# A decoder layer on one core: the triangular solve's transfers on other queues, and the solve one value tile later

## The chip, the cores and the metric

One Trainium2 chip, one of its cores. The metric is the device time of one execution in microseconds. The engines: TensorE (PE, with PEld for its weight loads), VectorE (DVE), ScalarE (ACT), GpSimd (POOL) and SyncE (SP), which here only issues transfers. Each engine works through its own list of instructions in order, and a transfer is issued by the engine in whose list it stands: an issue that has to wait holds up everything behind it in that list.

## The reference

One decoder layer over 256 tokens of width 2048, in float32. What the change touches is the RWKV-7 scan over 16 heads of width 64, and the rest stands around it.

```
h = rms_norm(x)
proj = h @ w_in                          # 2048 -> 4448 columns
r, k, v, w, a, g = split(token_shift(proj[:3360]))
# for each head, token by token:
sa    = state @ a_t                      # a = -kk, b = kk * a
state = state * w_t + sa b_t^T + v_t k_t^T
y_t   = state @ r_t
y = group_norm(y) + bonus;  y = y * g    # 16 groups of 64
y_mla = latent attention on the other columns (c_q, c_kv, k_pe)
x = x + concat(y, y_mla) @ w_out
x = x + gated MLP with a width-3 convolution (2048 -> 5632 -> 2048);  rms_norm
```

## The kernel before

All large products are done in two float32r parts: `piece` loads a 512 KB weight block by SP (`raw`, three buffers), ACT rounds it to `hi` (L133), DVE subtracts to get `lo` (L134), and PE multiplies both (L163 with `hi`, L166 with `lo`). A tile of the input projection (`in_tile`) is two such halves of 8 + 8 matmuls into one of three product banks `mm`. `joined` empties a bank: a copy on ACT (L171), an add on DVE (L172) and a scale on DVE (L173). The bank is free for PE behind L172.

The input projection runs tile by tile: key tiles 1 to 8, receptance tiles 9 to 16, value tiles 17 to 24, then latent tiles 27 to 34 (`latent`, two times four). A list `pend` holds small steps that are called after a tile, or after one more tile.

The scan is done in four chunks of 64 tokens. For each chunk and head a unit triangular system of 64 x 64 has to be inverted, which the kernel does for all 64 systems together, by halves of 32. `gram` builds the Gram blocks `G1` (PE L524, DVE L529) and stores the 32 x 32 diagonal blocks in DRAM (`dL`, 32 stores of 16 KB, L537). `solve_load` reads them back with one block row a partition (`Lp`, 512 KB, L566). `solve` multiplies `Lp` by the key norms (L575), and then solves on DVE with 31 steps of a multiply and an add (L579, L581) between which other DVE work stands. The inverse `Tq` goes to DRAM as `dT` (L583), its transposed copy `tp` as `dU` (L590), and from there back in the layouts that PE needs: `T11` (two loads, L592, in the profile `T`) and `TT` (four loads, L596); each of these has 1024 runs of 128 bytes. PE then makes the off-diagonal blocks: `pR` from `T11` and `G1` (L625), DVE scales it to `RT` (L629), `pT` from `RT` and `TT` (L638), copied back into `TT` (L642). Behind that comes the chain of chunks (`chunk`), whose matmuls `px`, `py`, `pS` (L674) alternate with small DVE and ACT steps, and which the scheduler fills up with the last latent tiles and the latent attention's products. Each half of the tokens then has a `group_norm`.

`rsqrt` runs on POOL unless an engine is given: 14 instructions there (L201 to L216), 11 on DVE. The group norms use it with 16 columns, `latent` with 2 (`ssm` L774, `rr` L776), behind the sum of squares `pss` (PE L772).

The order within each engine is made by a scheduler, which goes by its own costs and takes the program's order as a first wish; `tc.issue_after(i)` puts an instruction behind instruction i on its engine's list or by a wait.

Of the kernel before, what the change touches and what calls it, by code (L numbers as in the profile page):

```python
# [9 lines left out]
F32 = mybir.dt.float32  # L10
# [4 lines left out]
ALU = mybir.AluOpType  # L15
AX = mybir.AxisListType

P = 128
# [7 lines left out]
GN_EPS = 64e-5  # L26
# [28 lines left out]
def hybrid_layer(ctx: ExitStack, tc: tile.TileContext, a: dict, out: bass.AP):  # L55
    nc = tc.nc
    V, S, PE = nc.vector, nc.scalar, nc.tensor
# [4 lines left out]
    dr = ctx.enter_context(tc.tile_pool(name="dr", bufs=1, space=bass.MemoryType.DRAM))  # L62
# [3 lines left out]
    def nm(s):  # L66
        uid[0] += 1
        return f"{s}{uid[0]}"
# [28 lines left out]
    def ch(n="ch"):  # L97
        return ps.tile([P, 512], F32, tag="ch", name=nm(n), bufs=NCH)
# [4 lines left out]
    def con(shape, n, dt=F32):  # L103
        return sb.tile(shape, dt, name=n, bufs=1)
# [10 lines left out]
    def vv(name, i, rows=slice(0, P)):  # L115
        return vec[rows, VOFF[name] + i:VOFF[name] + i + 1]
# [28 lines left out]
                                               h.bitcast(F32), ALU.mult, ALU.subtract).ins  # L145
        return raw

    last_w, last_lo, last_x = [None], [None], [None]
    pend = []


    def flush(every=False):
        now = [f for n, f in pend if n == 0 or every]
        pend[:] = [(n - 1, f) for n, f in pend if n > 0 and not every]
        for f in now:
            f()
# [32 lines left out]
    def in_tile(i, pf=mm):  # L189
        acc = pf()  # L190
        for h in range(2):
            prod_b(acc, piece(a["win"][i, h]), x_hl, h * 8, 8, h == 0, h == 1)
        flush()
        return acc
# [174 lines left out]
    def shifted(acc, i, rows=slice(0, P), dst=None):  # L369
        h = t1("h", 257)  # L370
        nc.gpsimd.memset(h[rows, 0:1], 0.0)
        joined(h[rows, 1:257], acc, rsB, rows)
        o = t1("sh") if dst is None else dst
        S.activation(o[rows], h[rows, 1:257], AF.Copy, scale=om_mu[rows, i:i + 1])
        V.scalar_tensor_tensor(o[rows], h[rows, 0:256], vv("mu", i, rows), o[rows], ALU.mult, ALU.add)
        return o


# [65 lines left out]
    for p in range(8):  # L444
        pp, g = p // 2, p % 2
# [23 lines left out]
    Mp = con([P, 32], "Mp")  # L469
# [21 lines left out]
    dL = dr.tile([P, 32, 32], F32, name="dL")  # L491
    dLv = dL.rearrange("(h b c p) i t -> b c i h p t", h=2, b=2, c=4)
    boP = ch("boP")
    bon = con([64, 64], "bon")
    for p in range(8):
        pp, g = p // 2, p % 2
        acc = in_tile(9 + p)
        if p == 0:
            pend.append((0, key_norms_p))
        r = shifted(acc, 9 + p)  # L500
        rc = r.rearrange("p (c t) -> p c t", t=64)
        V.tensor_tensor(AR[pp][:, g, :, 1, :], rc, AR[pp][:, g, :, 1, :], ALU.mult)
        pr = t1("pr")
        V.tensor_tensor(pr.rearrange("p (c t) -> p c t", c=4), kv_(pp, g), AR[pp][:, g, :, 1, :], ALU.mult)

        def bonus(p=p, pr=pr):
            for w in range(2):
                PE.matmul(boP[:, w * 16 + p * 2:w * 16 + p * 2 + 2], pr[:, w * P:(w + 1) * P], brk[:, p, :],
                          start=True, stop=True)

        def gram(p=p, pp=pp):
            hf = p // 4
            e0 = (pp % 2) * 2
            for c in range(4):
                if pp % 2 == 0:
                    G1[c].append(s4(n="G1").rearrange("p (e t) -> p e t", e=8))
            for w in range(2):
                pg = [ch("pg") for _ in range(2)]
                for r in range(2):
                    for gg in range(2):  # L520
                        o = (r * 2 + gg) * P
                        for h in range(2):
                            hs = slice(h * 64, h * 64 + 64)
                            PE.matmul(pg[h][:, o:o + P], BK[pp][hs, gg, w * 2 + r, :, :],  # L524
                                      AR[pp][hs, gg, w * 2 + r, :, :], start=o == 0, stop=True,
                                      skip_group_check=True)
                for h in range(2):
                    for r in range(2):
                        V.tensor_tensor(G1[w * 2 + r][hf][:, h * 4 + e0:h * 4 + e0 + 2, :],  # L529
                                        pg[h][:, r * T:(r + 1) * T].rearrange("p (q t) -> p q t", q=2),  # L530
                                        gmask.unsqueeze(1).broadcast_to([P, 2, P]), ALU.mult)
            if pp % 2 == 1:
                for c in range(4):
                    for b in range(2):
                        r0 = 64 + b * 32
                        for h in range(2):
                            nc.sync.dma_start(dLv[b, c, :, h, hf * 4:hf * 4 + 4, :],  # L537
                                              G1[c][hf][r0:r0 + 32, h * 4:h * 4 + 4, b * 32:(b + 1) * 32])
            for c in range(3):
                if pp == 0:  # L540
                    BKt.append(s4(n="BKt").rearrange("p (a t) -> p a t", a=8))
                pt = ch("pt")
                for gg in range(2):
                    PE.transpose(pt[:, gg * P:(gg + 1) * P],
                                 BK[pp][:, gg, c, :, :].rearrange("p s t -> p (s t)"), ident)
                S.copy(BKt[c][:, pp * 2:pp * 2 + 2, :], pt[:, 0:T].rearrange("p (a t) -> p a t", a=2))

        pend.append((0, bonus))
        if g == 1:
            pend.append((0, gram))  # L550
# [8 lines left out]
    TT = con([P, 32, 64], "TT")  # L559
    T11 = []  # L560

    Lps = []

    def solve_load():
        Lps.append(sv("Lp").rearrange("p (i t) -> p i t", i=32))
        nc.sync.dma_start(Lps[0], dL)  # L566

    def solve():
        Lp = Lps[0]
        Tq = sv("Tq").rearrange("p (s t) -> p s t", s=32)  # L570
        tm = t1("tm")
        nc.gpsimd.memset(Tq, 0.0)
        nc.gpsimd.memset(Tq.rearrange("p s t -> p (s t)")[:, 0:1024:33], 1.0)
        nc.gpsimd.memset(TT, 0.0)
        V.tensor_tensor(Lp, Lp, Mp.unsqueeze(1).broadcast_to([P, 32, 32]), ALU.mult)  # L575
        for i in range(31):
            n, m = i + 1, 31 - i
            tv = tm[:, 0:n * m].rearrange("p (s t) -> p s t", s=n)
            V.tensor_tensor(tv, Tq[:, 0:n, i:i + 1].broadcast_to([P, n, m]),  # L579
                            Lp[:, i:i + 1, i + 1:32].broadcast_to([P, n, m]), ALU.mult)  # L580
            V.tensor_tensor(Tq[:, 0:n, i + 1:32], Tq[:, 0:n, i + 1:32], tv, ALU.add)  # L581
        dT = dr.tile([P, 32, 32], F32, name="dT")
        nc.sync.dma_start(dT, Tq)  # L583
        tp = sv("tp").rearrange("p (s t) -> p s t", s=32)
        V.tensor_copy(tp, Tq.rearrange("p s t -> p t s"))
        dU = dr.tile([2, 32, 32, 32], F32, name="dU")
        for h in range(2):
            T11.append(sv("T11").rearrange("p (q s) -> p q s", q=32))
        for h in range(2):
            nc.sync.dma_start(dU[h], tp[h * 64:h * 64 + 32])  # L590
        for h in range(2):
            nc.sync.dma_start(T11[h][64:96], dU[h].rearrange("q s t -> s q t"))  # L592
        for h in range(2):
            for b in range(2):
                k0 = h * 64 + b * 32
                nc.sync.dma_start(TT[k0:k0 + 32, :, b * 32:(b + 1) * 32], dT[k0:k0 + 32].rearrange("q s t -> s q t"))  # L596

    pend.append((0, solve_load))
    pend.append((1, solve))


    UV = [s4(n="UV").rearrange("p (e t) -> p e t", e=8) for _ in range(4)]
# [2 lines left out]
    for pp in range(4):  # L605
        vt = []
        for g in range(2):
            vt.append(shifted(in_tile(17 + pp * 2 + g), 17 + pp * 2 + g))
        pt = ch("pv")
        for g in range(2):  # L610
            for w in range(2):
                PE.transpose(pt[:, (g * 2 + w) * P:(g * 2 + w + 1) * P], vt[g][:, w * P:(w + 1) * P], ident)
        ptv = pt.rearrange("p (g w t) -> p g w t", g=2, w=2)
        for w in range(2):
            for r in range(2):
                S.copy(UV[w * 2 + r][0:64, pp * 2:pp * 2 + 2, :], ptv[r * 64:r * 64 + 64, :, w, :])
# [95 lines left out]
    def group_norm(w):  # L712
        y = yt[w]
        y3 = y.rearrange("p (h v) -> p h v", h=16)
        mu = st("gmu", 16)
# [4 lines left out]
        S.activation(sq, y, AF.Square)  # L720
        va = st("gva", 16)
        V.tensor_reduce(va, sq.rearrange("p (h v) -> p h v", h=16), AX.X, ALU.add)
        rv = rsqrt(va, 1.0 / 64, GN_EPS, 16)
        V.tensor_tensor(y3, y3, rv.unsqueeze(2).broadcast_to([P, 16, 64]), ALU.mult)
        V.tensor_tensor(y, y, gnwb[0], ALU.mult)
        V.tensor_tensor(y, y, gnwb[1], ALU.add)
# [165 lines left out]
    for half in range(2):  # L892
# [3 lines left out]
        for c in range(4):  # L896
# [9 lines left out]
            if half == 1:  # L906
# [3 lines left out]
                for j in range(2):  # L910
                    pt = ch("pxT").rearrange("p (k t) -> p k t", k=2)
                    for k in range(2):
                        for tb in range(2):
                            o = (j * 2 + k) * P
# [34 lines left out]
    for blk, nf in enumerate((24, 20)):  # L949
# [33 lines left out]
        for c in range(4):  # L983
            accs = [mm() for _ in range(2)]
            for i in range(n - (4 if blk == 1 and c == 3 else 0)):
                prod_a(accs, piece(a["wdn"][c, f0 // 2 + i]), h_hi, h_lo, i * 2, 2, i == 0, i == n - 1)
                if blk == 1 and i == 2:
                    q = n - 4 + c
                    held.append((q, piece(a["wdn"][3, f0 // 2 + q], a8("wt"))))
            for tb in range(2):  # L990
# [7 lines left out]
                o = tb * 4 + c  # L998
# [88 lines left out]
```

## Time and profile before

| | |
|---|---|
| median of 3 runs | 1209.64 us (1208.44 to 1210.07) |
| the profiled execution | 1207.02 us |
| its span in the trace | 1205.2 us |
| mean granted clock of TensorE | 0.987 |
| PE busy | 1161.3 us, 96% |
| DVE busy | 837.3 us, 69% |
| ACT busy | 598.2 us, 50% |
| POOL busy | 58.3 us, 5%, 206 instructions |
| moved by POOL's queue (software_dynamic) | 384 packets, 0.75 MB |
| the longest wait of PE | 7.3 us, a product (L163) on an eviction (L172) |

The profile is of one execution. A line of the timeline gives the start and the duration in microseconds, the engine, the source line, the operation with its output and inputs, how many there are together, and in brackets how long the engine had been idle and what ended the idle time. SPq, POOLq and ACTq are those engines' issues of transfers. A row of the waits has the total, the number and the longest.

### The profile page before, as it was taken

How to read it: one execution, taken by the hardware profiler on the slowest of the kernel's cores; microseconds unless marked ns; L12 is line 12 of the kernel's file. 1: busy time of each engine (PE TensorE's matmuls, PEld its weight loads, DVE VectorE, ACT ScalarE, POOL GpSimd, SP SyncE). 2: the span in 40 equal slices, each digit the busy share in tenths (PEclk: the TensorE clock that was granted, in tenths of full speed). 3: DMA queues.
4: the chain of work that ended last, by engine and by line, in shares of the span. 5: the costliest groups of instructions: out<-in, count | busy, mean ns of one | idle time of the engine just before them, and what ended most of it. 6: DMA issues, size and time to landing. Idle time of an engine off the chain costs nothing.

```text
span 1205.2 us, 18442 instructions
## 1 busy us (share of the span) xinstructions
PE 1161.3 (96%) x6993; PEld 992.1 (82%) x6993; DVE 837.3 (69%) x1360; ACT 598.2 (50%) x939; POOL 58.3 (5%) x206
## 2 busy tenths in 40 slices
PE   7899988998799999999999999999999999999996
PEld 6788877887677888888888888888888888888885
DVE  7798759977887556777777776444577777775563
ACT  6784435533444455655555554333355555554451
POOL 1500100011110001000000000000000000000000
PEclk9999998998899999999999999999999999999998
DMA  8544454654133555555555555555655555566661
GB/s 329 177 151 153 144 141 145 204 151 145 54 126 120 191 176 175 194 192 192 192 193 192 193 191 181 193 194 190 204 193 193 192 190 190 190 218 209 209 221 76
DMA packets 71017, 215.82 MB, mean 179 GB/s; under 512 B 17616, under 2 KB 17872, under 8 KB 70928
## 3 DMA queue, kind: packets, MB, share of 16 engines
q1 hardware_dynamic: 69776, 211.84, 53.5%
q10 hardware_dynamic: 768, 2.05, 0.5%
q8 instruction: 55, 0.90, 0.3%
q0 software_dynamic: 384, 0.75, 0.3%
q14 instruction: 34, 0.28, 0.1%
HBM read 210.48 MB, written 3.41 MB: 177 GB/s over the span
## 4 chain that ended last, share of the span: by engine, by line
PE 88%; DVE 7%; POOL 2%; issue 1%; DMA 1%; ACT 0%; SPq 0%; ACTq 0%; DVEq 0%; POOLq 0%
PE mm L163 36%; PE mm L166 18%; PE mm L185 9%; PE mm L183 9%; PE mm L184 9%; DVE lo L134 1%; PE pg L524 1%; PE py L674 1%; PE px L674 1%; POOL sinR L292 0%; DMA raw<-in_win 0%; DMA Lp<-dL 0%; POOL cosR L288 0%; DVE tw L415 0%; PE pS L674 0%
## 5 line engine op out<-in xcount | busy, mean ns | idle before, releaser
L134 DVE TENSOR_TENSOR lo<-raw,hi 128x1024 fp32r<-128x1024 f32 x376 | 460.3, 1225 | 286.6 <-ACT hi L133 277.5
L133 ACT CAST hi<-raw 128x1024 fp32r<-128x1024 f32 x376 | 395.0, 1051 | 458.0 <-issue 250.2
L163 PE MATMUL mm<-z,hi 128*128 128x512 f32 x1408 | 351.3, 392 | 0.0
L163 PEld LDWEIGHTS mm<-z,hi 128*128 128x128 f32 x1408 | 251.9, 188 | 43.7
L166 PEld LDWEIGHTS mm<-z,lo 128*128 128x128 f32 x1408 | 188.3, 188 | 14.5
L166 PE MATMUL mm<-z,lo 128*128 128x256 f32 x1408 | 191.6, 278 | 0.0
L163 PE MATMUL mm<-x,hi 128*128 128x512 f32 x528 | 142.2, 406 | 20.0 <-DVE h L172 12.0
L184 PE MATMUL mm<-lo,hh 128*128 128x512 f32 x336 | 130.7, 389 | 0.0
L185 PE MATMUL mm<-hi,hl 128*128 128x512 f32 x336 | 130.7, 389 | 0.0
L163 PEld LDWEIGHTS mm<-x,hi 128*128 128x128 f32 x528 | 95.8, 193 | 37.5 <-ACT hi L133 8.0
L183 PE MATMUL mm<-hi,hh 128*128 128x512 f32 x336 | 119.7, 389 | 0.0
L166 PEld LDWEIGHTS mm<-x,lo 128*128 128x128 f32 x528 | 73.6, 191 | 7.0 <-issue 1.0
L166 PE MATMUL mm<-x,lo 128*128 128x256 f32 x528 | 78.9, 285 | 0.0
L185 PEld LDWEIGHTS mm<-hi,hl 128*128 128x128 f32 x336 | 63.1, 188 | 13.2
L184 PEld LDWEIGHTS mm<-lo,hh 128*128 128x128 f32 x336 | 63.1, 188 | 13.0
L183 PEld LDWEIGHTS mm<-hi,hh 128*128 128x128 f32 x336 | 63.1, 188 | 13.0
L184 PE MATMUL mm<-lo,yhi 128*128 128x512 f32 x128 | 51.1, 399 | 0.0
L185 PE MATMUL mm<-hi,ylo 128*128 128x512 f32 x128 | 50.5, 394 | 0.0
L183 PE MATMUL mm<-hi,yhi 128*128 128x512 f32 x128 | 49.6, 405 | 0.0
L961 POOL MEMSET gt<- 128x2 f32 x44 | 4.3, 100 | 575.9 <-DVE hl L973 572.8
L185 PEld LDWEIGHTS mm<-hi,ylo 128*128 128x128 f32 x128 | 24.1, 188 | 5.5 <-DVE ylo L746 0.4
L183 PEld LDWEIGHTS mm<-hi,yhi 128*128 128x128 f32 x128 | 23.9, 188 | 5.7 <-DVE kn L172 0.8
(290 smaller groups left out, 1124.2 us busy)
## 6 DMA issues: line engine op xcount, KB each, us to landing
raw<-in_wgu SPq DMA_DIRECT2D x176, 512.0 KB, 3.3
raw<-in_wdn SPq DMA_DIRECT2D x88, 512.0 KB, 4.1
raw<-in_win SPq DMA_DIRECT2D x70, 512.0 KB, 4.0
raw<-in_wout SPq DMA_DIRECT2D x32, 512.0 KB, 3.3
raw<-in_wuq SPq DMA_DIRECT2D x6, 512.0 KB, 4.2
xraw<-in_xT SPq DMA_DIRECT2D x4, 512.0 KB, 6.2
xt<-in_x SPq DMA_DIRECT2D x4, 512.0 KB, 6.6
raw<-in_wuv SPq DMA_DIRECT2D x4, 512.0 KB, 3.3
```

The costliest lines, as they stand in the source:

```text
L133: S.copy(hi, raw)
L134: last_lo[0] = V.tensor_tensor(lo, raw, hi.bitcast(F32), ALU.subtract).ins
L163: PE.matmul(acc, hi[:, j * P:(j + 1) * P], act(kt0 + j), start=first and j == 0, stop=False, skip_group_check=True)
L166: PE.matmul(acc[:, :T], lo[:, j * P:(j + 1) * P], act(kt0 + j)[:, 0, :], start=False, stop=last and j == n - 1, skip_group_check=True)
L183: PE.matmul(accs[tb], ah, wh, start=first and j == 0, stop=False)
L184: PE.matmul(accs[tb], ah, wl, start=False, stop=False)
L185: PE.matmul(accs[tb], al, wh, start=False, stop=last and j == n - 1)
L524: PE.matmul(pg[h][:, o:o + P], BK[pp][hs, gg, w * 2 + r, :, :], AR[pp][hs, gg, w * 2 + r, :, :], start=o == 0, stop=True, skip_group_check ...
L674: PE.matmul(dst[HS[h], a_ * 64:(a_ + 1) * 64], lhsT, rhs, start=n == 0 and a_ == 0, stop=True, skip_group_check=True)
L961: nc.gpsimd.memset(gt[:, 0:2], 0.0)
```

## The change

Five edits:

1. The 32 stores of `dL` are issued by POOL and no longer by SP.
2. The load of `Lp` stays with SP, and is put behind the last weight load that the program has made by then.
3. The multiply of `Lp` is put behind the final DVE step of the last `shifted` tile. `solve` is no longer called by `pend` but by the value loop, right after tile 18, the second value tile.
4. The seven transfers of the factors move from SP to POOL, in the order `dU` twice, `dT`, `T11` twice, `TT` four times.
5. The group norms' rsqrt moves from POOL to DVE.

```
-            nc.sync.dma_start(dLv[b, c, :, h, hf * 4:hf * 4 + 4, :],
+            nc.gpsimd.dma_start(dLv[b, c, :, h, hf * 4:hf * 4 + 4, :],
...
     def solve_load():
-        nc.sync.dma_start(Lps[0], dL)
+        with tc.issue_after(last_w[0]):
+            nc.sync.dma_start(Lps[0], dL)
...
-        V.tensor_tensor(Lp, Lp, Mp.unsqueeze(1).broadcast_to([P, 32, 32]), ALU.mult)
+        with tc.issue_after(last_sh[0]):
+            V.tensor_tensor(Lp, Lp, Mp.unsqueeze(1).broadcast_to([P, 32, 32]), ALU.mult)
...
-        nc.sync.dma_start(dT, Tq)
         V.tensor_copy(tp, Tq.rearrange("p s t -> p t s"))
...
         for h in range(2):
-            nc.sync.dma_start(dU[h], tp[h * 64:h * 64 + 32])
+            du = nc.gpsimd.dma_start(dU[h], tp[h * 64:h * 64 + 32]).ins
+        with tc.issue_after(du):
+            nc.gpsimd.dma_start(dT, Tq)
         for h in range(2):
-            nc.sync.dma_start(T11[h][64:96], dU[h].rearrange("q s t -> s q t"))
-        for h in range(2):
-            for b in range(2):
-                k0 = h * 64 + b * 32
-                nc.sync.dma_start(TT[k0:k0 + 32, :, b * 32:(b + 1) * 32], dT[k0:k0 + 32].rearrange("q s t -> s q t"))
+            t11 = nc.gpsimd.dma_start(T11[h][64:96], dU[h].rearrange("q s t -> s q t")).ins
+        with tc.issue_after(t11):
+            for h in range(2):
+                for b in range(2):
+                    k0 = h * 64 + b * 32
+                    nc.gpsimd.dma_start(TT[k0:k0 + 32, :, b * 32:(b + 1) * 32],
+                                        dT[k0:k0 + 32].rearrange("q s t -> s q t"))
     pend.append((0, solve_load))
-    pend.append((1, solve))
...
             vt.append(shifted(in_tile(17 + pp * 2 + g), 17 + pp * 2 + g))
+            if pp == 0 and g == 1:
+                solve()
...
-        rv = rsqrt(va, 1.0 / 64, GN_EPS, 16)
+        rv = rsqrt(va, 1.0 / 64, GN_EPS, 16, V)
```

The change also moves work that it doesn't name, since the scheduler orders every engine anew. In the pieces below a number behind a name tells one buffer's use from another's; the lines of the changed kernel lie 1 to 7 higher than before.

On DVE, where the multiply of `Lp` stands, before (`h_1904<-mm_1776` is the eviction of tile 18):

```order
L134 TENSOR_TENSOR lo_2062<-raw_2059,hi_2061 128x1024
L134 TENSOR_TENSOR lo_2093<-raw_2090,hi_2092 128x1024
L575 TENSOR_TENSOR Lp_1766<-Lp_1766,Mp 128x1024
L579 TENSOR_TENSOR tm_1822<-Tq_1821,Lp_1766 128x31
L581 TENSOR_TENSOR Tq_1821<-Tq_1821,tm_1822 128x31
L172 TENSOR_TENSOR h_1904<-mm_1776,h_1904 128x256
```

and now (`h_1966<-mm_1921` is the eviction of tile 19):

```order
L134 TENSOR_TENSOR lo_2062<-raw_2059,hi_2061 128x1024
L134 TENSOR_TENSOR lo_2093<-raw_2090,hi_2092 128x1024
L134 TENSOR_TENSOR lo_2115<-raw_2112,hi_2114 128x1024
L134 TENSOR_TENSOR lo_2155<-raw_2152,hi_2154 128x1024
L578 TENSOR_TENSOR Lp_1766<-Lp_1766,Mp 128x1024
L582 TENSOR_TENSOR tm_1830<-Tq_1829,Lp_1766 128x31
L584 TENSOR_TENSOR Tq_1829<-Tq_1829,tm_1830 128x31
L172 TENSOR_TENSOR h_1966<-mm_1921,h_1966 128x256
```

The eviction of tile 18 has moved ahead of this piece; two more splits and the eviction of tile 19 now stand where it stood.

On SP, the load of `Lp` among the weight loads, as the difference of the two lists (- before, + now):

```order
-L537 DMA dL<-G_1541 32x4x32 x2
-L537 DMA dL<-G_1542 32x4x32 x3
 L127 DMA raw_2112<-in_win 128x1024
 L127 DMA raw_2152<-in_win 128x1024
-L566 DMA Lp_1766<-dL 128x1024
 L127 DMA raw_2174<-in_win 128x1024
 L127 DMA raw_2205<-in_win 128x1024
 L127 DMA raw_2227<-in_win 128x1024
+L568 DMA Lp_1766<-dL 128x1024
```

The stores are gone from this list, and the load has moved back by three weight loads. The last of those goes into the raw buffer that `lo_2155` reads.

The transfers of the factors, before on SP:

```order
L583 DMA dT<-Tq_1821 128x1024
L590 DMA dU<-tp_1891 32x1024 x2
L127 DMA raw_3257<-in_win 128x1024
L596 DMA TT<-dT 32x32x32
L592 DMA T_1894<-dU 32x32x32
L592 DMA T_1895<-dU 32x32x32
L596 DMA TT<-dT 32x32x32 x3
```

and now on POOL, among the rsqrt of the first latent:

```order
L210 TENSOR_TENSOR rt_3068<-ry_3067 128x2
L592 DMA dU<-tp_1897 32x1024 x2
L594 DMA dT<-Tq_1829 128x1024
L211 TENSOR_TENSOR rt_3068<-rt_3068,rm_3066 128x2
L596 DMA T_1901<-dU 32x32x32
L215 TENSOR_SCALAR rt_3068<-rt_3068 128x2
L596 DMA T_1902<-dU 32x32x32
L216 TENSOR_TENSOR ry_3067<-ry_3067,rt_3068 128x2
L601 DMA TT<-dT 32x32x32 x4
L210 TENSOR_TENSOR rt_3068<-ry_3067 128x2
```

They have left SP's weight loads, and the rest of the rsqrt stands behind them. DVE's copy `tp`, which `dU` reads, stood 5.6 us ahead of PE's `pss` in the trace before and stands right behind the copy `ssm` of `pss` now; PE has three half tiles between `pss` and `pR` where it had one and a half.

More of the change, by code (lines that the diff above doesn't have):

```diff
@@ L146, in xsplit @@
         return raw
-    last_w, last_lo, last_x = [None], [None], [None]
+    last_w, last_lo, last_x, last_sh = [None], [None], [None], [None]
     pend = []
@@ L374, in shifted @@
         S.activation(o[rows], h[rows, 1:257], AF.Copy, scale=om_mu[rows, i:i + 1])
-        V.scalar_tensor_tensor(o[rows], h[rows, 0:256], vv("mu", i, rows), o[rows], ALU.mult, ALU.add)
+        last_sh[0] = V.scalar_tensor_tensor(o[rows], h[rows, 0:256], vv("mu", i, rows), o[rows],
+                                            ALU.mult, ALU.add).ins
         return o
@@ L581, in solve @@
             V.tensor_tensor(Tq[:, 0:n, i + 1:32], Tq[:, 0:n, i + 1:32], tv, ALU.add)
-        dT = dr.tile([P, 32, 32], F32, name="dT")
-        nc.sync.dma_start(dT, Tq)
         tp = sv("tp").rearrange("p (s t) -> p s t", s=32)
@@ L586, in solve @@
         dU = dr.tile([2, 32, 32, 32], F32, name="dU")
+        dT = dr.tile([P, 32, 32], F32, name="dT")
         for h in range(2):
```

## Prediction

> **What bounds the kernel now.** I read the page first, then TensorE's waits, then the timeline around the longest of them, then the hand-over of the solved factors, the windows behind it, and the transfers by tile.
>
> ```profile
> PE 1161.3 (96%) x6993; PEld 992.1 (82%) x6993; DVE 837.3 (69%) x1360; ACT 598.2 (50%) x939; POOL 58.3 (5%) x206
> PE 88%; DVE 7%; POOL 2%; issue 1%; DMA 1%; ACT 0%; SPq 0%; ACTq 0%; DVEq 0%; POOLq 0%
> PE mm L163 <- DVE h L172: 12.0, 4, 7.3
> PE px L674 <- DVE XB L685: 5.4, 5, 2.7
> PE mm L166 <- DVE lo L134: 2.1, 1, 2.1
> ```
>
> TensorE (PE) is busy for 96% of the span, so the change can win only in PE's few gaps, and loses wherever it makes a new one. The waits (total, times, longest) show the one large gap: a weight product waits 7.3 us for a tile's eviction at L172. The timeline around it:
>
> ```profile
> 175.89 1.07 PE L166 MATMUL mm<-x,lo 128*128 128x256 f32 x7
> 176.94 0.33 SPq L566 DMA_DIRECT2D Lp<-dL  x1
> 177.06 1.23 DVE L134 TENSOR_TENSOR lo<-raw,hi 128x1024 fp32r<-128x1024 f32 x1 [1.92 <-PE mm L166]
> 178.31 12.93 SPq L127 DMA_DIRECT2D raw<-in_win  x2
> 182.09 1.23 DVE L575 TENSOR_TENSOR Lp<-Lp,Mp 128x1024 f32<-128x1024 f32 x1 [3.81 <-DMA Lp<-dL]
> 184.22 3.78 PE L163 MATMUL mm<-x,hi 128*128 128x512 f32 x8 [7.26 <-DVE h L172]
> 187.80 1.40 PE L166 MATMUL mm<-x,lo 128*128 128x256 f32 x8
> ```
>
> PE stops at 176.96. VectorE (DVE) splits one more weight piece (to 178.29), and stands before the multiply of `Lp` until its load, issued at 176.94, has landed. Only behind that multiply comes the eviction that frees a product bank. PE resumes at 184.22, and the 3.78 us of its first eight products is a slow clock after the gap.
>
> **1. The stall moves one tile on.** On DVE the evictions of tile 18 now stand ahead of the multiply, but so do two more splits, and the eviction of tile 19 stands behind it. With three product banks, PE does one more tile and then waits for tile 19's bank. On SyncE (SP) the load of `Lp` now stands behind three more weight loads. The last of them needs the raw buffer that the split directly ahead of the multiply reads, and that split needs the buffer that PE frees at the end of its last tile. So the load can't go out early. From PE's stop: split 1.33 (176.96 to 178.29), weight load and step to the next 0.4 (the 0.33 row), landing 5.1 (176.94 to 182.09 with the multiply's start), multiply to PE's restart 2.13 (182.09 to 184.22). Sum 9.0 against 7.26: **+1.7 us**. With the least that the load could take, 3.5 as the `T` loads below, it is about 0; the slow clock behind it I leave as it is.
>
> **2. Stores on GpSimd (POOL).** The rows by tile are count, then min/median/max ns of an issue; the next block has KB and median us to landing.
>
> ```profile
> L805 POOL DMA_DIRECT2D qs<-qr x4: 489/496/536, 284.8 to 286.3; - x4
> L434 POOL DMA_DIRECT2D ksw<-kraw x4: 503/503/549, 47.3 to 48.8; - x4
> L432 POOL DMA_DIRECT2D kraw<-kraw x1: 607/607/607, 46.7 to 46.7; - x1
> L247 POOL DMA_DIRECT2D rp<-in_pos x1: 763/763/763, 1.3 to 1.3; - x1
> L537 SPq DMA_DIRECT2D dL<-G x32: 303/424/1719, 133.0 to 175.2; - x32
> L592 SPq DMA_DIRECT2D T<-dU x2: 564/637/710, 240.4 to 241.0; - x2
> L596 SPq DMA_DIRECT2D TT<-dT x4: 316/638/747, 240.0 to 243.3; - x4
> ```
> ```profile
> dL<-G SPq DMA_DIRECT2D x32, 16.0 KB, 1.6
> TT<-dT SPq DMA_DIRECT2D x4, 128.0 KB, 4.0
> dU<-tp SPq DMA_DIRECT2D x2, 128.0 KB, 4.4
> T<-dU SPq DMA_DIRECT2D x2, 128.0 KB, 3.5
> rp<-in_pos POOLq DMA_DIRECT2D x1, 32.0 KB, 6.4
> ```
>
> A `dL` store has 128 runs, as `in_pos` has: 0.76 us of POOL each. The last sixteen need 12.2 us, from about 168.2 (the evictions of most Gram blocks) to 180.4, and have landed by 181 to 186 (1.6 to 6.4 from the last one's start). The load of `Lp` goes out at about 176.96 + 5.8 + 1.7 = 184.5, so they are mostly hidden: 0, at most +1.5. SP's saved issue time gains nothing, since PE does not wait for weights there.
>
> **3. The hand-over of the factors.** The timeline before the change (start, duration):
>
> ```profile
> 234.74 1.14 DVE L585 COPY tp<-Tq 128x1024 f32<-128x1024 f32 x1
> 240.33 0.50 PE L772 MATMUL pss<-ones,css 128*128 128x2 f32 x4
> 240.69 2.09 PE L163 MATMUL mm<-x,hi 128*128 128x512 f32 x8
> 241.85 0.15 DVE L774 COPY ssm<-pss 128x2 f32<-128x2 f32 x1
> 243.57 2.01 PE L163 MATMUL mm<-x,hi 128*128 128x512 f32 x8
> 245.50 0.31 PE L625 MATMUL pR<-T,G 32*32 32x32 f32 x4
> 246.17 2.21 PE L625 MATMUL pR<-T,G 32*32 32x32 f32 x124
> 247.64 1.41 DVE L629 TENSOR_TENSOR RT<-pR,mtok 32x512 f32<-32x512 f32 x2
> 251.50 3.93 PE L638 MATMUL pT<-TT,RT 32*32 32x32 f32 x128
> ```
>
> The copy `tp` was done 4.5 us ahead of `pss`; now DVE's order has it right behind `ssm`, which needs `pss`. Call PE's start of `pss` X. PE then has three half tiles of 2.88 (240.69 to 243.57) and reaches `pR` at X + 9.1. `tp` ends at X + 0.5 + 0.15 + 1.14 = X + 1.8, the two `dU` stores (32 runs, 0.5 each) and `dT` follow on POOL, and the first `dU` has landed at X + 6.25 (4.4). Then come, on the same queue, two `T11` loads and four `TT` loads of 1024 runs each. What POOL takes to issue one, d, the trace does not show. The lower bound is SP's 0.64 for the same transfer; the upper is POOL's own trend drawn straight: 32, 64 and 128 runs took 0.50, 0.61 and 0.76, some 2.7 ns a run, so 3.2 us. That trend flattens (3.3 ns a run, then 2.4); if each doubling goes on so (1.8, 1.35, 1.0 ns), 1024 runs take 0.76 + 0.23 + 0.34 + 0.51 = **1.85 us**. I take that: POOL is the engine that will issue, and it is between the bounds.
>
> The second `T11` lands at X + 6.25 + 2d + 2.9 (3.5 less SP's issue). The second `TT` lands at X + 6.45 + 4d + 3.4, the fourth 2d later. `RT` is ready 2.7 after `pR` starts (half of 2.5 and 1.41), and nothing else stands on PE between. So with d = 1.85: `pR` starts at 12.85 (wait 3.75) and ends at 15.35; `pT` waits for the second `TT` at 17.25 (1.9), and its next quarter, due at 18.45, for the fourth at 20.95 (2.5). Sum **+8.15**. With 0.64 the same steps give 1.3 + 0.2 = 1.5; with 3.2 they give 6.45 + 4.6 + 5.2 = 16.25. The Trainium skill, "DMA: Bandwidth & Descriptors", section "Anatomy of one DMA — SWDGE (gpsimd) path", says that one can emit a lot of descriptors before the incremental cost shows up; by that d would be the lower value and the sum 6.65 less. The POOL rows from 32 to 128 runs already show an increment, so I do not follow it.
>
> **4. The chain behind it, and the group norms.** The windows (busy us of PE, its weight loads, DVE, ACT, POOL; granted clock) and the rows of the first group norm:
>
> ```profile
> 262.00:300.00 38.00, 32.89 (x486) 28.55 (x486) 27.84 (x59) 14.91 (x32) 5.09 (x18) 0.92 0.43 140
> 300.00:335.00 35.00, 27.88 (x317) 21.52 (x314) 27.74 (x41) 14.49 (x27) 5.11 (x14) 0.89 0.20 65
> 310.01 2.45 DVE L729 TENSOR_TENSOR gsq<-UV,bon 64x1024 f32<-64x1024 f32 x2
> 310.07 1.23 POOL L201 TENSOR_SCALAR rm<-gva 128x16 f32<-128x16 f32 x1 [23.32 <-DVE gva L722]
> 312.61 0.21 POOL L210 TENSOR_TENSOR rt<-ry 128x16 f32<-128x16 f32 x1
> 316.29 1.23 DVE L724 TENSOR_TENSOR yt<-yt,ry 128x1024 f32<-128x1024 f32 x1 [2.07 <-POOL ry L216]
> 321.22 0.96 PE L166 MATMUL mm<-cl,lo 128*128 128x256 f32 x4 [2.09 <-DVE lo L134]
> ```
>
> In the windows the scan's chain leaves PE 5.1 and 7.1 us idle. The chain starts behind `pT`, and PE's program now holds three half tiles between `pss` and `pR` and not one and a half, so 4.3 us less work lies beside the chain. The chain's waits are only part of those windows, so I take a third, **+1.5** (0 to 4.3). The group norm's rsqrt leaves POOL for eleven DVE instructions of about 0.17 (`ssm` has 0.15), 1.9 us, and takes away DVE's wait of 2.07: **0** (the wait gone and half hidden, -3; all on the path, +2).
>
> **Sum**: 1.7 + 0 + 8.15 + 1.5 + 0 = 11.35. The profiled execution took 1207.02 (span 1205.2 and 1.82 around it), so 1218.4 by its measure; the median of the three runs, 1209.64, is 2.62 above it: **1221.0**. No change means within 0.2%, 2.4 us, about what a measurement here can tell.
>
> **Rivals.**
> *Issue is cheap on POOL* (SP's 0.64): the hand-over costs 1.5, the sum is 4.7, 1214.3. For it speaks that 1024 runs cost SP only twice what its cheapest issue does; against it the POOL rows.
> *Issue grows straight* (3.2): the hand-over costs 16.25, 1229.1, and with a slow clock after two gaps as long as that of 177, 2 us more: 1231.
> *POOL is held up by DVE.* `rm` above took 1.23 on POOL, where a like instruction takes 0.21, while DVE ran L729 beside it. If issues are held up by 1 us too, sixteen stores take 28 us from 168.2, the last lands near 198 to 200, not before 184.5: +15, and seven factor transfers take up to 7 more: 1235 to 1243. The Trainium skill, "SBUF — State Buffer", section "SBUF: two separate sides", describes such starvation of GpSimd's descriptor writes, but under DVE's fast copy modes; the rows here show a held-up POOL instruction, and no held-up issue.
> *The chain's gaps fill: faster.* At 262 to 335 PE idles 12.2 us at a clock of 0.9 (another 5.7 at full speed). If the new order and DVE's rsqrt halve both, -9.0; it wins only if the hand-over and the stall stay under 6.6 together, so with d below about 1.2. At 0.64: -9.0 + 1.7 + 1.5, 1203.8. Against it: less work stands beside the chain, not more.
> *Nothing to be seen*: the `Lp` load lands in 3.5, the issue is cheap, and the chain hides the rest: 1209.6 to 1212.
>
> **How the numbers follow.** Forecast 0.42 (own range 1214 to 1229); cheap issue 0.20; straight growth 0.12; POOL held up 0.06; gaps fill 0.11; nothing 0.09. Slower is the first four, 0.80; faster 0.11; same 0.09. From 1208 to 1233 leaves out the faster case, POOL held up, and little else.
>
> **What would show it.** Right: PE's wait for L172 at about 183, some 9 us long, `Lp` issued after 184; POOL issues of `T` and `TT` near 1.85 us; a wait of `pR` of 2 to 6 us, and waits of `pT`. Wrong: no wait at `pR` and issues under 0.8 (cheap issue); a stall at L172 under 5 us; stores that take over 1.2 us each; less than 8 us of PE idle between the hand-over's end and the second group norm.

## The result and the profile after

The changed kernel takes 1224.87 us (median of 4, 1223.13 to 1225.27) against 1209.66 before: slower by 1.25%, ratio 1.0125 with a 95% interval of 1.0107 to 1.0142. The forecast was 1221.0 in a range of 1208 to 1233. The profiled executions took 1223.13 and 1207.02, their spans 1221.3 and 1205.2, so there are 16.1 us to find.

TensorE's waits after the change (total, times, longest), without that of the first product of all for its weights, 8.0 us before and 8.4 after:

```profile
PE mm L163 <- DVE h L172: 13.0, 5, 8.6
PE pR L632 <- DMA T<-dU: 6.5, 2, 6.2
PE px L681 <- DVE XB L692: 5.3, 4, 2.7
PE pyT L749 <- DVE yt L745: 3.4, 1, 3.4
```

The wait for an eviction is still there and longer, and a new one stands at `pR`, for the `T` loads. Where the 16.1 us arose shows when the span is cut at events of TensorE that both kernels have: the last Gram products, the first `pss`, the first `pS`. The windows of before (length, then busy us and instructions of PE, its weight loads, DVE, ACT, POOL; granted clock; transfers):

```profile
164.92:240.33 75.41, 68.15 (x404) 59.64 (x404) 61.58 (x130) 38.64 (x67) 0.39 (x4) 0.95 0.56 168
240.33:264.87 24.54, 24.54 (x386) 21.36 (x385) 16.53 (x26) 6.81 (x10) 3.71 (x14) 1.00 0.66 167
264.87:1205.20 940.33, 916.44 (x5301) 781.08 (x5300) 628.38 (x918) 452.97 (x690) 25.16 (x104) 0.99 0.54 179
```

and after:

```profile
165.33:242.64 77.31, 68.74 (x403) 60.24 (x403) 59.61 (x126) 37.94 (x65) 10.15 (x24) 0.93 0.51 155
242.64:281.34 38.70, 32.19 (x387) 28.72 (x385) 17.95 (x28) 7.13 (x10) 11.67 (x23) 0.74 0.46 123
281.34:1221.30 939.96, 917.20 (x5301) 782.11 (x5300) 632.01 (x940) 453.38 (x690) 14.81 (x76) 0.99 0.55 179
```

PE does the same number of instructions in each window, but for one, so the lengths can be compared: +0.4 ahead of the first, +1.9 up to `pss`, **+14.2 from `pss` to `pS`**, and -0.4 over all the rest. In the middle window PE is idle for 6.51 us (38.70 - 32.19), and its busy time itself grew by 7.65 us (32.19 - 24.54) at a clock of 0.74. So less than half of the 14.2 us is waiting; the rest is the same work at a slower clock. Other traces whose order is that of the change in the stretch in question tell how firm this is: from `pss` to `pS` they took 38.71 (load_pool) and 38.76 (rsqrt_pool), but up to `pss` 76.28 to 77.09, and only_factors, with the order of before, took 76.68. So the 14.2 is firm, and the 1.9 is hardly more than the spread. (These runs are described below.)

The stall in the timeline after the change:

```profile
181.99 1.10 PE L166 MATMUL mm<-x,lo 128*128 128x256 f32 x8
183.27 1.22 DVE L134 TENSOR_TENSOR lo<-raw,hi 128x1024 fp32r<-128x1024 f32 x1 [1.56 <-ACT hi L133]
185.14 0.33 SPq L568 DMA_DIRECT2D Lp<-dL  x1
189.52 1.23 DVE L578 TENSOR_TENSOR Lp<-Lp,Mp 128x1024 f32<-128x1024 f32 x1 [5.03 <-DMA Lp<-dL]
191.18 0.42 DVE L172 TENSOR_TENSOR h<-mm,h 128x256 f32<-128x256 f32 x1
191.66 3.78 PE L163 MATMUL mm<-x,hi 128*128 128x512 f32 x8 [8.57 <-DVE h L172]
```

PE stops at 183.1, DVE ends its split at 184.5 and waits 5.03 us for `Lp`, which SyncE could issue only at 185.14. PE resumes 8.57 us later; 9.0 had been worked out, with 5.1 for a landing that took 4.4.

The hand-over after the change:

```profile
242.64 0.50 PE L779 MATMUL pss<-ones,css 128*128 128x2 f32 x4
243.26 1.11 DVE L586 COPY tp<-Tq 128x1024 f32<-128x1024 f32 x1
243.44 0.99 POOL L201 TENSOR_SCALAR rm<-ssm 128x2 f32<-128x2 f32 x1 [43.54 <-DVE ssm L781]
244.51 1.04 POOL L205 TENSOR_SCALAR ry<-rm 128x2 int32<-128x2 int32 x1
246.13 1.08 POOL L592 DMA_DIRECT2D dU<-tp  x2 [0.30 <-issue]
247.21 0.55 POOL L594 DMA_DIRECT2D dT<-Tq  x1
250.21 0.82 POOL L596 DMA_DIRECT2D T<-dU  x1 [2.23 <-DMA dU<-tp]
251.25 0.81 POOL L596 DMA_DIRECT2D T<-dU  x1
257.88 0.42 PE L632 MATMUL pR<-T,G 32*32 32x32 f32 x4 [6.20 <-DMA T<-dU]
258.60 3.51 PE L632 MATMUL pR<-T,G 32*32 32x32 f32 x122 [0.31 <-DMA T<-dU]
262.01 3.49 PE L645 MATMUL pT<-TT,RT 32*32 32x32 f32 x62
271.31 3.76 PE L163 MATMUL mm<-x,hi 128*128 128x512 f32 x8
```

An issue of a 1024-run load took GpSimd 0.82 us, not the 1.85 of the forecast. But `T` landed late. Its rows after the change (an issue's ns, min/median/max; then us to landing):

```profile
L596 POOL DMA_DIRECT2D T<-dU x2: 813/815/817, 250.2 to 251.2; - x2
DMA to landing us min/median/max: 7.3/7.5/7.6
```

Before it was 3.3/3.5/3.7. The 122 products of `pR` took 3.51 us, where 124 had taken 2.21. The clock stays down for long, as windows cut at `pR`, at the first large product and behind it show:

```profile
257.88:271.31 13.43, 13.12 (x277) 12.63 (x277) 7.00 (x13) 0.05 (x1) 1.72 (x9) 0.50 0.24 42
271.31:276.28 4.97, 4.97 (x18) 4.20 (x18) 2.12 (x5) 1.79 (x3) 0.00 (x0) 0.54 0.00 0
276.28:281.34 5.06, 5.06 (x42) 4.06 (x40) 2.71 (x3) 1.42 (x2) 0.00 (x0) 1.00 0.31 104
```

For 13.4 us PE is almost always busy with small matmuls (`pR`, `pT`, the first `px`, and at the end four of 128 x 128), at a clock of 0.50; it takes 5 us of large products to get it back.

### The profile page after: what moved, and what is told of

The parts are those of the page before. It is cut to its first block, busy times and chain, and to the rows that moved or that the text cites. A ratio compares the mean times of both kernels' runs of the same rounds, so it can differ in the third digit from the quotient of the medians.

```text
span 1221.3 us, 18450 instructions
## 1 busy us (share of the span) xinstructions
PE 1170.0 (96%) x6993; PEld 1000.7 (82%) x6993; DVE 841.7 (69%) x1382; ACT 598.9 (49%) x939; POOL 72.8 (6%) x219
## 4 chain that ended last, share of the span: by engine, by line
PE 89%; DVE 5%; DMA 2%; POOL 1%; issue 1%; ACT 1%; SPq 0%; ACTq 0%; DVEq 0%; POOLq 0%
PE mm L163 36%; PE mm L166 18%; PE mm L185 9%; PE mm L184 9%; PE mm L183 9%; PE pg L525 1%; DVE lo L134 1%; PE px L681 1%; DMA xt<-in_x 1%; DMA T<-dU 1%; PE pT L645 1%; DMA raw<-in_win 1%; PE py L681 0%; POOL cosR L288 0%; DVE tw L416 0%
```

## The experiments

My theory was now: (A) the loss sits in the hand-over, because `T`'s transfers land late among other traffic, and PE then does `pR` and `pT` at half speed because it stood still; the stall at `Lp` hangs on the load's place in SyncE's list. The rival (B): the copy `tp`, which moved behind `ssm`, or GpSimd's queue as such, is to blame. Ratios are to the kernel before, run on the same chip.

**factors_sp: the factor transfers back on SyncE.**

```
-            du = nc.gpsimd.dma_start(dU[h], tp[h * 64:h * 64 + 32]).ins
+            nc.sync.dma_start(dU[h], tp[h * 64:h * 64 + 32])
...
```

`dT`, `T11` and `TT` go the same way, in the order of the kernel before.

> The changed kernel with the seven factor transfers back on SyncE in their old order, all else as changed (stores on GpSimd, the load of Lp late on SyncE, the solve behind tile 18, rsqrt on VectorE). Theory A: the loss behind pss is the landing of the software transfers (7.5 us for T where SyncE's took 3.5) and the slow clock after the gap that it makes. Then T lands about 4 us sooner, the wait of pR falls from 6.5 to about 1.5 us, the clock stays up, and the time is 1211 to 1214 us. Theory B: the loss is that the copy tp now stands behind ssm, whichever engine issues. Then the wait of pR stays at 5 us or more and the time at 1221 us or more.

Measured: 1211.51 us, ratio 1.0018 (1.0008 to 1.0029); the changed kernel's was 1.0125. A holds by the time. B's first half falls, since `tp` still stands behind `ssm`; whether GpSimd's queue as such is slow, this run can't tell, and dt_last_hold does. The window from `pss` to `pS` and `pR` in the timeline:

```profile
242.12:268.71 26.59, 26.07 (x387) 22.77 (x385) 17.65 (x28) 6.59 (x10) 5.37 (x14) 0.94 0.69 191
```
```profile
252.47 0.31 PE L629 MATMUL pR<-T,G 32*32 32x32 f32 x4
253.60 2.21 PE L629 MATMUL pR<-T,G 32*32 32x32 f32 x124
```

26.59 us for 38.70, and no recorded wait of `pR`. `T` took 5.6 us to land, though, 2 less than in the change and not 4; what helped more by these times is that SyncE issued it sooner, 4.1 us behind the start of `pss` (246.26 - 242.12) and not 7.6 (250.21 - 242.64).

**only_factors: the kernel before with the factor transfers alone on GpSimd.**

```
-        nc.sync.dma_start(dT, Tq)
...
+            du = nc.gpsimd.dma_start(dU[h], tp[h * 64:h * 64 + 32]).ins
...
```

The other factor transfers are as in the change.

> The kernel before with nothing changed but the factor transfers, which are issued by GpSimd in the new order. VectorE copies tp some 4.5 us ahead of pss here. Theory A: the first dU store goes out 4.3 us ahead of pss, T lands 3.4 + 0.8 + 7.5 later, at about 7.4 us behind the start of pss, and PE comes to pR at about 4.7: a wait of 2 to 3 us, 1212 to 1217 us by whether the clock falls. Theory B (only the late tp costs): no wait of pR over 1 us and a time within 2.4 us of the kernel before.

Measured: 1216.99 us, ratio 1.0067 (1.0044 to 1.0091), at the upper edge of A; so this part alone is enough for half of the loss, with `tp` early, and a late `tp` can't be all of it. The wait came at another place than expected, at `pT` for `TT`, 2.7 us in two; the `TT` loads took 6.7 to 10.2 us to land. The profiled execution's stall at L172 was also longer, 8.1 us, because `Lp` took 6.1 to land; most of what it is longer lies in the window from `pss` to `pS`, 31.12 us against 24.54.

**fill: eight matmuls that do nothing, ahead of `pR`.** They fill PE's gap; the profile shows them as 16 records.

```
+    fill = ch("fill")
+    for _ in range(8):
+        PE.matmul(fill, ident, Lps[1].rearrange("p s t -> p (s t)")[:, 0:512], start=True, stop=True)
```

> The changed kernel with eight added matmuls ahead of pR (identity by 512 columns of tp in float32, into a bank that nothing reads), some 7 us of PE work that adds nothing to the result. Theory A: of the 14 us lost behind pss half is the wait and half is the clock that stays at half speed through pR and pT because PE stood still ahead of them. With the gap filled PE does as much in the same time and keeps its clock: 1215 to 1219 us, pR and pT at full speed (124 of pR in about 2.2 us). Theory B: only the wait counts, and pR and pT are slow for another reason, such as the data: the added work takes the wait's place and the time stays at 1223 to 1227 us, or rises if the added work is longer than the wait.

Measured: 1220.04 us, ratio 1.0094 (1.0076 to 1.0112), by the ratios 0.3% faster than the changed kernel, with 7 us of work more. It missed A's range by 1 us, and B's by 3. In the timeline:

```profile
248.50 7.03 PE L628 MATMUL fill<-tp,cst 128*128 128x512 f32 x16
258.85 2.21 PE L637 MATMUL pR<-T,G 32*32 32x32 f32 x126 [0.81 <-DMA T<-dU]
```
```profile
243.76:279.79 36.03, 34.56 (x404) 27.28 (x402) 17.92 (x28) 7.16 (x10) 10.88 (x23) 0.91 0.44 132
```

`pR` runs at full speed again: its slowness was the clock and not the data. Without the filler PE is busy for 27.53 us here (34.56 - 7.03) against 24.54 before and 32.19 in the changed kernel, so 4.7 of the 7.65 us are recovered; 3.0 us stay, at a mean clock of 0.91 in this window. The filler moved one more thing: SyncE issued the next weight load (`in_wuv`) at 258.37 only, and the first `T`, with `dT` beside it, landed in 4.5 us, the second in 3.2. `pR` began only 1.2 us sooner than in the change all the same, 14.0 us behind the start of `pss`, and the most of it waited for the second `T`, which went out at 255.59.

**dt_last: `dT` behind the two `T` loads. dt_last_hold: besides, the weight loads held back until `T` has landed.**

```
-        with tc.issue_after(du):
-            nc.gpsimd.dma_start(dT, Tq)
...
         with tc.issue_after(t11):
+            nc.gpsimd.dma_start(dT, Tq)
```
```
+        for h in range(2):
+            hold = nc.sync.dma_start(dS[h:h + 1], T11[h][64:65, 0, :]).ins
...
```

In the second kernel the first two loads of `in_wuv` are issued behind `hold`.

> The changed kernel with one transfer moved: dT (512 KB) is issued behind the two T loads and not ahead of them. Theory A: T lands 7.5 us after its issue because it shares the transfer engines with dT and with the weight loads that SyncE now sends at the same time; without dT it lands in 3.5 to 6 us and the wait of pR falls from 6.5 to between 2 and 5 us, while TT lands later and pT waits 3 to 7 us for it: 1220 to 1228 us. Theory B: a load of 1024 runs from GpSimd's queue takes 7 us or more by itself: the landing of T and the wait of pR stay.

> As dt_last, and besides two small stores of a row of each T11 on SyncE, which wait until T has landed and so hold back the weight loads of in_wuv behind them. Nothing of size then runs beside the T loads. Theory A: T lands in 3 to 4 us as on SyncE before, pR waits 1 to 2.5 us. Theory B: it still lands 7 us or more after its issue. The time, with pT waiting for TT as in dt_last, 1218 to 1226 us under A; no less than 1224 under B.

Measured: 1224.38 us, ratio 1.013 (1.0105 to 1.0155), and 1219.61 us, ratio 1.0091 (1.0066 to 1.0115), from two executions each. The rows of `T`, issue and landing, first without the hold, then with it (there the landing row also counts the two small stores of `T`):

```profile
L594 POOL DMA_DIRECT2D T<-dU x2: 802/804/806, 249.6 to 251.5; - x2
DMA to landing us min/median/max: 5.8/6.1/6.3
```
```profile
L594 POOL DMA_DIRECT2D T<-dU x2: 802/804/806, 250.4 to 253.1; - x2
DMA to landing us min/median/max: 3.2/3.6/4.0
```

The same load from the same queue takes 7.5 us beside `dT` and the weight loads of `in_wuv`, 6.1 without `dT`, 3.6 or so without either: as fast as SyncE's. With `dT` and without those weight loads (the first `T` in fill) it took 4.5. So the late landing comes of what runs beside it, the weight loads above all, and not of GpSimd's queue. The Trainium skill, "DMA: Bandwidth & Descriptors", section "Issuing engines are not separate DMA queues", says that transfers of all issuing engines run on the same DMA engines and interleave; these rows agree. On SyncE before, the weight loads had stood behind the factor transfers in one list and waited with them, which kept the way free. SyncE's issues before, in the change and in dt_last_hold (`T` goes out at 240.37, 250.21 and 250.45):

```profile
241.79 2.11 SPq L596 DMA_DIRECT2D TT<-dT  x3
243.94 1.11 SPq L127 DMA_DIRECT2D raw<-in_win  x1
```
```profile
250.37 3.11 SPq L127 DMA_DIRECT2D raw<-in_wuv  x2
```
```profile
256.66 0.83 SPq L127 DMA_DIRECT2D raw<-in_wuv  x2
```

Some of what was expected did not come. In dt_last `T`'s landing and `pR`'s wait of 5.8 us lie a little above A's bounds, and still below B's; in dt_last_hold `pR` waited 4.3 us and not 1 to 2.5, since the second `T` went out 2.7 us behind the first (253.13), when the second `dU` had landed. dt_last's wait at `pT` did not come as a recorded wait: PE did other products there, and `pT` came at 271.74.

**load_pool: the load of `Lp` on GpSimd, behind the stores.**

```
-        with tc.issue_after(last_w[0]):
-            nc.sync.dma_start(Lps[0], dL)
+        nc.gpsimd.dma_start(Lps[0], dL)
```

> The changed kernel with the load of Lp issued by GpSimd right behind the stores, and so no longer behind three weight loads on SyncE. VectorE's order around the multiply is the same. Theory A: the stall of PE behind tile 21 hangs on the load's place in SyncE's list. The stores have landed by 179.3, the load goes out then and lands 4.4 to 7.5 us later, the multiply starts at 184.5 to 186.8 and not at 189.5, and the stall falls from 8.6 to 3.6 to 6 us: 1219 to 1222.5 us. Theory B: the load's place does not matter, since the multiply waits for something else: the stall stays above 8 us and the time at 1225.

Measured: 1220.06 us, ratio 1.0096 (1.0075 to 1.0116). The stall:

```profile
181.86 0.56 POOL L567 DMA_DIRECT2D Lp<-dL  x1 [3.72 <-DMA dL<-G]
186.80 1.23 DVE L577 TENSOR_TENSOR Lp<-Lp,Mp 128x1024 f32<-128x1024 f32 x1 [0.62 <-DMA Lp<-dL]
188.94 3.23 PE L163 MATMUL mm<-x,hi 128*128 128x512 f32 x7 [4.16 <-DVE h L172]
```

8.57 became 4.16 as expected, and DVE waits 0.62 us for the load, not 5.03. The hand-over stayed at 38.71 us (238.71 to 277.42), so the two losses are apart from each other here.

**stores_sp: the stores back on SyncE.**

```
-                            nc.gpsimd.dma_start(dLv[b, c, :, h, hf * 4:hf * 4 + 4, :],
+                            nc.sync.dma_start(dLv[b, c, :, h, hf * 4:hf * 4 + 4, :],
```

> The changed kernel with the 32 stores back on SyncE, all else as changed. The scheduler then puts the load of Lp one weight load after raw_2112 as in the kernel before, and VectorE's multiply one split earlier, still ahead of tile 19's eviction; tp and pR move one more tile of products back. Theory A (the stall hangs on the load's place in SyncE's list): the load goes out near 177 and lands near 182, PE stops near 183 and the stall falls from 8.6 to 2 to 4 us; pR, which PE reaches 17 us behind pss, finds T there and the clock stays up: 1209 to 1217 us. Theory B: the stall stays over 7 us or pR still waits over 4 us: 1219 us or more.

Measured: 1215.5 us, ratio 1.0053 (1.0037 to 1.007). The scheduler now sets the load earlier in SyncE's list (it goes out at 178.52 and not at 185.14), the stall is small, and the window up to `pss` is 70.24 us and not 77.31; `pR` still waits, though it stands a tile further back:

```profile
187.17 3.26 PE L163 MATMUL mm<-x,hi 128*128 128x512 f32 x8 [2.39 <-DVE h L172]
254.46 0.31 PE L632 MATMUL pR<-T,G 32*32 32x32 f32 x4 [0.40 <-DMA T<-dU]
256.96 3.46 PE L632 MATMUL pR<-T,G 32*32 32x32 f32 x121 [2.20 <-DMA T<-dU]
```

A wait of 2.6 us, and `pR` and `pT` slow again (121 of `pR` in 3.46 us): I had expected the clock to stay up. The window from `pss` to `pS` is 33.55 us, with PE idle for 4.02 and busy for 4.99 more than before.

**rsqrt_pool: the group norms' rsqrt back on GpSimd.** The edit is `rsqrt(va, 1.0 / 64, GN_EPS, 16)`.

> The changed kernel with the group norms' rsqrt back on GpSimd, all else as changed. Theory A: as in the prediction, this edit is worth nothing: from the first pS on the two kernels took 940.3 and 940.0 us, so the time stays within 2.4 us of the changed kernel, 1222.5 to 1227. Theory B: rsqrt on VectorE hid a loss of the later chain, and without it the time rises to 1228 or more; or it was itself a loss, and the time falls to 1221 or less.

Measured: 1224.11 us, ratio 1.0133 (1.0118 to 1.0148): no difference from the changed kernel.

**solve_only: stores and factor transfers both on SyncE,** so of the change the solve behind tile 18, the placing of the load, and rsqrt on DVE are left.

> The changed kernel with the stores and the factor transfers both back on SyncE: what is left of the change is the solve behind tile 18, the load put behind the last weight load, and rsqrt on VectorE. Theory A: the solve's new place is a gain by itself (a stall of 2.4 us at L172 as in stores_sp, some 5 us less than before up to pss), and the hand-over is 28 to 31 us, since pR stands a tile further back as in best2 and the transfers do not make PE wait; what is left of the chain is 2 us slower. Together 1207 to 1212 us, within the noise of the kernel before. Theory B: the solve's place is what costs, whatever the queues: 1214 us or more.

Measured: 1210.8 us, ratio 1.0009 (0.9997 to 1.0022). Its windows are 70.08 us up to `pss`, 30.68 up to `pS` and 942.92 behind it: 5.3 us less than before, then 6.1 and 2.6 more. So with the stores on SyncE the solve's new place is a gain up to `pss`, and it is given away behind it. There the trace shows `pR` a tile further back, with the large products ahead of it and none left between it and `pS`:

```profile
235.80:266.48 30.68, 25.75 (x386) 23.06 (x385) 19.18 (x35) 6.60 (x10) 4.42 (x14) 0.85 0.63 171
```

PE is idle for 4.9 us of this window, and was for none of it before. No run shows by itself that `pR`'s place is the reason.

With the rest of the change in place, four kernels hold the two moves of transfers apart. Against the kernel before, solve_only with neither is 0.1% slower, factors_sp with the stores alone 0.2%, stores_sp with the factor transfers alone 0.5%, and the change with both 1.25%. Together they cost far more than each by itself: the stores on GpSimd cost almost nothing beside factor transfers on SyncE, and 0.7% beside those on GpSimd.

**best1, best2, best3: looking for a version that is faster.** All three have the stores and the load of `Lp` on GpSimd and the factor transfers on SyncE in their old order. best2 calls `solve` after tile 19, best3 has rsqrt on GpSimd.

```
-            if pp == 0 and g == 1:
+            if pp == 1 and g == 0:
```

> Both remedies together: stores on GpSimd, the load of Lp on GpSimd right behind them, the factor transfers back on SyncE in their old order, the solve behind tile 18 and rsqrt on VectorE. If the two costs add up, the stall is 4.2 us as in load_pool (4.3 less than changed, and a shorter slow clock) and the hand-over 26.6 us as in factors_sp: 1211.5 - 5 = 1205 to 1208 us, a little under the kernel before. Rival: an earlier solve only lets PE come sooner to pR and wait there, and the time stays at 1210 or more.

> As best1, with the solve behind tile 19, one tile later, so that the load of Lp has landed when VectorE comes to its multiply. Theory: no stall at L172 over 1 us, 4 us and the slow clock behind it less than in best1, while the factors come 2 us later and pR stands one more tile of products back: 1202 to 1207 us. Rival: the scan's chain, which begins later with less work beside it, gives the gain back: 1206 to 1210 us.

> As best1 (stores and the load of Lp on GpSimd, factor transfers on SyncE, solve behind tile 18) with the group norms' rsqrt on GpSimd. By theory A of rsqrt_pool it is as fast as best1 within 2 us, 1205.5 to 1209.5; if rsqrt on VectorE costs what the longer wait of pyT shows (3.4 us in best1, 2.0 before), 1 to 2 us faster than best1.

Measured: best1 1207.32 us, ratio 0.9983 (0.9972 to 0.9994); best2 1213.64, ratio 1.0037 (1.0023 to 1.005); best3 1210.7, ratio 1.0003 (0.999 to 1.0016). best1's windows up to `pss` and up to `pS`:

```profile
165.41:237.08 71.67, 67.69 (x403) 59.21 (x403) 59.44 (x126) 37.89 (x65) 10.71 (x25) 0.98 0.54 168
237.08:263.68 26.60, 26.08 (x387) 22.74 (x386) 17.65 (x28) 6.58 (x10) 5.34 (x14) 0.94 0.71 193
```

The two remedies add up as worked out: 3.7 us less than before up to `pss`, 2.1 more behind it. best1 is 0.17% faster than the kernel before; its interval leaves out 1, but it is one of three tries, and the forecast held 0.2% for what a measurement can tell, so this is no sure gain. best2 is slower than either case had it, and keeps a stall, one tile further on than best1's. Its row, and its window from `pss` to `pS`:

```profile
193.16 3.75 PE L163 MATMUL mm<-x,hi 128*128 128x512 f32 x8 [3.54 <-DVE tm L581]
```
```profile
238.53:269.19 30.66, 25.74 (x386) 23.06 (x384) 19.93 (x38) 6.58 (x10) 3.81 (x14) 0.86 0.66 172
```

`Lp` had landed by 185.5 (issued at 180.9, 4.6 us), so it is not the load: the multiply stands behind a split that starts only when PE has stopped (189.62), and from there split, multiply and eviction alone take the 3.5 us (1.32 to the multiply's start at 190.94, 2.22 from there to PE's restart). A later place only moves that gap on. The larger part of best2's loss lies behind it: 30.66 us from `pss` to `pS` against best1's 26.60, with `pR` a tile further back as in solve_only, and 943.31 against 940.02 from there on. best3 is 1.2 us above its range; its interval and best1's just overlap, so whether rsqrt's engine matters there stays open, and in the changed kernel it made no difference.

## Why the prediction was right, and where it was not

- *The stall moves one tile on.* Right in mechanism, and the stall's length in size: 8.57 us against 9.0, and 8.4 to 8.9 in the five other traces that share the order. That it cost 1.9 us up to `pss` against 1.7 is closer than the spread of the traces can vouch for. load_pool shows that the load's place in SyncE's list makes half of it.
- *Stores on GpSimd cost nothing on the path.* Right for the issue: they took 0.55 us each (0.76 was taken), and the last one went out at 176.54, well ahead of the load at 185.14. But the stores' move is not free: without them on SyncE the scheduler puts the load of `Lp` later, and with them back the stall is 2.39 us and not 8.57 (stores_sp). The sum has that cost under the stall; that it hangs on the stores had not been seen.
- *The hand-over, +8.15.* This step failed, and it holds most of the loss. Its sum came from the term d, an issue of 1.85 us on GpSimd. Measured: 0.82 for `T` and 0.78 for `TT`, near the lower bound. The last point of the curve that gave 1.85 was a single issue, the load of `in_pos` with 0.76 us for 128 runs; the 32 stores with as many runs took 0.55. In its place stand three things that were not in the sum. The landing took 7.5 us where 2.9 + d = 4.75 was taken, because `dT` and the weight loads ran beside it (dt_last, dt_last_hold). `dU` went out at 3.5 us behind the start of `pss` and not at 1.85, since `rm` and `ry`, ahead of it on GpSimd, took 0.99 and 1.04 us (0.18 and 0.19 before) while DVE ran `tp` and a split. And 7.65 us of slow clock were left out. The two waits at `pT` that d made did not come. That 8.15 was not further from 14.2 is luck, two errors against each other: a cheaper issue, and a later landing with a slower clock. With 0.82 for d the prediction's own steps give an estimate of 2 us (a wait of 1.7 at `pR`, 0.3 behind it), and the sum would have led to about 1215.
- *The chain, +1.5.* Nothing was lost there: 939.96 us against 940.33. The 4.3 us less of products beside it did no harm. Where `pR` stood another tile back there was a loss, 942.92 in solve_only and 943.30 in stores_sp.
- *The group norm, 0.* Right within what the runs can tell (rsqrt_pool).
- *The rivals.* Cheap issue was right on the issue and wrong on the time, since it held the landing to be SyncE's. Straight growth fell. "POOL is held up by DVE" was half right: two of its small instructions ahead of `dU` took 0.8 us longer each beside DVE, and no issue is seen to have been held up. The Trainium skill, "SBUF — State Buffer", section "SBUF: two separate sides", tells of descriptor writes that starve under DVE's fast copy modes. The change's trace does not show that: issues of one kind hardly differed, 813 to 817 ns for `T`, but none of these ran beside a copy. Faster by filled gaps fell: PE's idle time behind `pS` hardly changed (23.9 us before, 22.8 after).

By terms the sum would have been 1.9 + 14.2 - 0.4, and 0.4 ahead of the first window, = 16.1 us, against the 11.35 forecast. The time lay inside a wide range, and the path, a second gap at `pR`, was foreseen; how long it would be, and the slow clock behind it, were not.

## What to carry to other kernels

When transfers leave a shared issue queue, ask what that queue had held back: here the weight loads had waited behind the factor loads, and set free they ran beside them and, with `dT`, doubled the landing of what TensorE was waiting for. A gap ahead of small matmuls can cost twice its length, when they run on at half clock until large products come: 6.5 us of idle time brought 7.7 of slower work in the change, 4.0 brought 5.0 in stores_sp. And a load that is to end a stall must be placed ahead of what the stall itself holds up, which only the order of the issuing queue shows.

## What the runs showed of the hardware

- The half clock lasted through 13.4 us of nearly unbroken matmuls (0.50), most of them 32 x 32, and went only behind 5 us of products of full size. After the stall at `Lp`, with full products at once, the clock was 0.50 in the first 5 us and 0.93 in the next 5 (191.66 to 201.66), and 0.58 and 1.00 before the change (184.22 to 194.22), from which the half clock is estimated to have lasted 5.7 and 4.2 us. The same small matmuls ran at full speed where they came warm (before, fill). The Trainium skill, "TensorE: Matmul & The Clock Gate", section "Part 1: The HAM clock gate", says that some 4 us of sustained matmul activity release the throttle; the stall before agrees, the one after took longer, and `pR` and `pT` show that being busy with such matmuls was not enough here.
- An issue on GpSimd took 0.55 us for 128 runs of 128 bytes and 0.82 for 1024: eight times the runs for half as much again.
